# Low parts of four weight chunks: adding DMA transfers onto ScalarE's negative high parts instead of VectorE's subtraction

## The chip, the cores and the metric

The kernel runs on one core of a Trainium2 chip. The metric is the device time of one execution in microseconds (us), given as the median of several runs. TensorE (PE) multiplies matrices; VectorE (DVE), ScalarE (ACT) and GpSimd (POOL) do elementwise work; SyncE (SP) issues transfers. Each of these has an instruction queue of its own that runs in order and waits on semaphores. Transfers issued by SP, ACT or POOL are carried out by 16 DMA engines.

## The reference

A decoder trunk of two layers on 256 tokens with width 1024, in float32:

```
for layer in (0, 1):
    h = h + 0.5 * swiglu(rms_norm(h), ffn1)     # 1024 -> 2816 -> 1024
    h = h + mixer[layer](rms_norm(h))
    h = h + 0.5 * swiglu(rms_norm(h), ffn2)
out = rms_norm(h) * final_norm
swiglu(x) = (silu(x @ w_gate) * (x @ w_up)) @ w_down
```

The first layer's mixer joins a dilated window attention and a spatial gating. The second layer's is an attention with 16 heads of 64; with 256 tokens and blocks of 256 it is plain causal attention. Its output is projected by `c_w_out` (1024 x 1024), and the last FFN (`ffn2` of layer 1) follows.

## The kernel before

**Arithmetic.** A float32 value `x` is used as a high part `hi`, which is `x` rounded to the matmul format float32r, and a low part `lo = x - hi`. Each product is three matmuls (`mm3`, L283 to L285): high by high, and two of high by low. TensorE does little else than these, 7617 matmuls.

**Weights.** All weight matrices are cut into 165 chunks of up to 128 x 2048 float32 (1024 KB). `Stream` carries each through three steps: `load_one` (L146) has SP load it into one of three `raw` tiles; `split_parts` makes `whi` (ScalarE, a copy that rounds, L188) and `wlo` (VectorE, `raw - whi`, L189), in two halves of 1024 columns for an ordinary chunk; then TensorE uses both. `whi` and `wlo` have four buffers each (`SPL`). A `raw` tile is free for the next load when the last instruction that reads it is done.

**Order.** The program is written in the order in which TensorE wants its work, and a scheduler orders the instructions of each engine by that order and by its own estimate of when they are ready. Where a split shouldn't come before something else on its engine, the code says so: `hold` stops splitting, `release(tc, behind, one)` lets one chunk or all go, with an edge that puts its instructions behind the given ones on the same engine, and `split_first` starts a chunk with its first half alone.

**The second mixer's end.** In `c_mixer` a table of slots puts scores, turned probabilities and weighted sums between the projection's matmuls. The scores are masked and reduced on VectorE (L788, L803), exponentiated on ScalarE (L806), scaled by VectorE (L813), turned by TensorE (L822), split into `pth` (ScalarE) and `ptl` (VectorE, L288), and multiplied with the values; `mixh` and `mixl` (L836, L838) are the result's two parts. `project` multiplies them with four chunks of `c_w_out`: two that hold two row blocks over all columns, then two that hold the last four row blocks over one half of the columns. The splits of the latter two, and of the next FFN's first gate and up chunk, are placed by

```
slots.at((23,), lambda _: st.release(tc, [*weighted(4), *put_ks[7]], True))
slots.at((25,), lambda _: st.release(tc, weighted(5), True))
slots.at((27,), lambda _: st.split_first(tc, turn(15)))
slots.at((29,), lambda _: st.release(tc, weighted(7)))
```

After the projection `Next.pair` adds each pair of column blocks to the residual (L329), and makes the next FFN's input `xTh` (ScalarE, L319) and `xTl` (VectorE, L322). The FFN's first chunk is used in the order `TURNS`: row blocks 0 to 3, then 4 and 5, then 6 and 7; the second in plain order. ScalarE also issues a load of the final norm's gains (`fg`, L539) at the FFN's start, and POOL has the power of the root (L291) some time later.

Of the kernel before, what the change touches and what calls it, by code (L numbers as in the profile page):

```python
# [10 lines left out]
F32 = mybir.dt.float32  # L11
F32R = mybir.dt.float32r
AF = mybir.ActivationFunctionType
ALU = mybir.AluOpType
# [22 lines left out]
LINE, SHIFT = 64, 16  # L37
EDGE, GAP = 56, 240

RESET, RESHIFT = 3, 52  # L40
DOWN = ((0, 8), (8, 8), (16, 6))
MIX1, MIX2 = (4, 5, 6, 7, 0, 1, 2, 3), (0, 1, 2, 3, 4, 5, 6, 7)


def weight_chunks():

    chunks = []

    def add(m, r, n, c0, c1, shift=0, cuts=(), reset=0):
        chunks.append((m[:-1], m[-1], r, n, c0, c1, shift, cuts, reset))  # L50

    def cols(m, c0, w, cuts=(), reset=0):
        n = CH // w
        for k in range(0, KD, n):
            add(m, k * 128, n, c0, c0 + w, SHIFT if w == 256 else 0, cuts, reset)

    def ffn(name, layer, last=False, again=(2, 3)):
        first = len(chunks)
        for c in range(0, FF, 256):
            if len(chunks) == 0:  # L60
                for k in (0, 4):
                    add((f"{name}_w_gate", f"{name}_w_up", layer), k * 128, 4, c, c + 256, SHIFT,
                        (1, 2, 3) if k else (0.5, 1, 2, 3))
                continue
            for m in ("gate", "up"):
                n = len(chunks)
                cuts = (6,) if first == 0 and n in again else ()
                cols((f"{name}_w_{m}", layer), c, 256, cuts, RESET if n - first in again else 0)
        wd = (f"{name}_w_down", layer)
        if last:  # L70
            for k in range(0, FT, 2):
                add(wd, k * 128, 2, 0, D)
            return
        for c in range(0, D, 256):
            for k, n in DOWN:
                add(wd, k * 128, n, c, c + 256, SHIFT)

    def mix(m, order):
        for k in order[:4:2]:
            add(m, k * 128, 2, 0, D, SHIFT)  # L80
        for c in (0, 512):
            add(m, order[4] * 128, 4, c, c + 512, SHIFT)

    ffn("ffn1", 0, again=(2,))
    wab = ("ab_w_in", 0)
    cols(wab, 0, 256)
    cols(wab, 512, 256, reset=RESET)
    cols(wab, 1024, 512)
    cols(wab, 2048, 512)
    for c, n in ((1536, RESET), (1792, 0), (256, RESET), (768, RESET)):  # L90
        cols(wab, c, 256, reset=n)
    mix(("ab_w_out", 0), MIX1)
    ffn("ffn2", 0, again=(2,))
    ffn("ffn1", 1, again=())
    wc = ("c_w_in", 0)
    for c in range(4):
        cols(wc, c * 256, 256, reset=RESET if c % 2 else 0)
        cols(wc, 1024 + c * 256, 256, reset=0 if c else RESET)
        if c % 2 == 0:
            cols(wc, 2048 + c * 256, 512)  # L100
    mix(("c_w_out", 0), MIX2)
    ffn("ffn2", 1, True, again=(2,))
    return chunks


def loads_of(j):

    return 4 if j < 2 else 2 if j < 4 else 1
# [12 lines left out]
class Stream:  # L121
# [7 lines left out]
        self.held = False  # L129
        self.begun = None  # L130

    def add(self, nk, w, shift, cuts, reset):

        cuts = (*(cuts or (() if reset else (nk / 2,))), nk)
        self.specs.append((nk, w, loads_of(len(self.specs)), shift, cuts, reset))

    def load_one(self, between=lambda i: None):
        j = self.loaded
# [24 lines left out]
    def split_parts(self):  # L163
        j = self.split
        nc = self.nc
        nk, w, _, shift, cuts, reset = self.specs[j]
        raw = self.raws.pop(j)
        his, los = (p.tile([128, CH + LINE], F32R, name=m) for p, m in ((self.hi_pool, "whi"), (self.lo_pool, "wlo")))

        h = w // 2  # L170
        far = nk * w - reset * h + RESHIFT // LINE * LINE + RESHIFT

        def at(k):
            return int(k * w) - reset * h + shift

        def part(t, k):
            if k >= reset:
                return t[:, at(k) : at(k) + w]
            return Halves(*(t[:, a : a + h] for a in (far + k * h, shift + k * h)))

        self.parts[j] = tuple([part(t, k) for k in range(nk)] for t in (his, los))

        def split(a, r):
            n = r.free_size()
            hi, lo = his[:, a : a + n], los[:, a : a + n]
            if len(r.shape) == 3:
                hi, lo = (t.rearrange("p (k c) -> p k c", k=reset) for t in (hi, lo))
            nc.scalar.activation(hi, r, AF.Copy)  # L188
            nc.vector.tensor_sub(lo, r, hi.bitcast(F32))  # L189

        if reset:
            r = raw[:, : reset * w].rearrange("p (k c) -> p k c", k=reset)
            split(far, r[:, :, :h])
            split(shift, r[:, :, h:])
        k0 = reset
        for k1 in cuts:
            split(at(k0), raw[:, int(k0 * w) : int(k1 * w)])
            k0 = k1
            yield
        self.split += 1  # L200
# [40 lines left out]
def trunk(ctx: ExitStack, tc: tile.TileContext, a, out):  # L241
# [15 lines left out]
    for ms, _, _, n, c0, c1, *how in weight_chunks():  # L257
        st.add(n, len(ms) * (c1 - c0), *how)
# [798 lines left out]
def _layout(a):  # L1057

    def tiles(m):
        return m.reshape(-1, 128, m.shape[-1]).transpose(1, 0, 2)  # L1060

    chunks = weight_chunks()
    weights = np.zeros((len(chunks), 128 * CH), np.float32)
    for j, (ms, layer, r, n, c0, c1, *_) in enumerate(chunks):
        w = np.concatenate([a[m][layer, r : r + n * 128, c0:c1] for m in ms], axis=1)
        if j >= len(chunks) - FT // 2:
            w = w[:, ROWS]
        w = tiles(w).reshape(128, loads_of(j), -1).transpose(1, 0, 2)
        weights[j, : w.size] = w.ravel()
    norms = np.stack([a[n] for n in ("ffn1_norm", "mix_norm", "ffn2_norm")]).reshape(-1, 128)  # L1070
    x = np.zeros((KD // 2, 128, XW), np.float32)
    for i, to in enumerate(x):
        to[:, 16:] = tiles(a["x"][0].T)[:, 2 * i : 2 * i + 2].reshape(128, -1)
        to[:, :2] = norms[2 * i : 2 * i + 2].T
    pieces = x[0][:, :XFIRST], x[0][:, XFIRST:], x[1:]
    return {
        "x": np.concatenate([v.ravel() for v in pieces]),
        "norms": norms.T[:, KD:],
        "weights": weights,
        "spatial": a["ab_w_spatial"][0].transpose(2, 0, 1),  # L1080
        "ab_v_norm": a["ab_v_norm"],
        "ab_b_spatial": a["ab_b_spatial"],
        "final_norm": a["final_norm"][ROWS],
        "consts": _constants(),
    }
# [19 lines left out]
```

## Time and profile before

| | |
|---|---|
| median of 3 runs | 933.38 us (933.0 to 934.26) |
| the profiled execution | 933.77 us, of it the span of the profile 932.1 us |
| granted TensorE clock | 1.00 |
| busy: PE, DVE, ACT, POOL | 923.5, 631.2, 504.6, 76.4 us |
| DMA | 176.99 MB, 190 GB/s over the span |

A row of a timeline gives the start and the duration in us, the engine, the source line, the operation, what is written from what, how often, and in square brackets the engine's idle time before it with the instruction that ended it. A row of the waits gives who waited for whom, the sum in us, the number of times, and the longest. A row of the groups gives busy time and mean duration in ns, then the idle time before. The chain that ended last gives shares of the span.

### The profile page before, as it was taken

To read this page: it belongs to the slowest core of one execution; us is meant where nothing else is said; L and a number is where in the kernel's file an instruction comes from. 1 tells how busy PE (TensorE), PEld (TensorE's weight loads), DVE (VectorE), ACT (ScalarE), POOL (GpSimd) and SP (SyncE) were. 2 spreads that over 40 slices of the span, in tenths; PEclk is the share of its full clock that TensorE was granted. 3 is DMA by queue.
4 is the path that set the end of the run, shared out by engine and by line. 5 is a ranking of instruction groups with operands and counts; after the bars stand their busy time and mean duration, and the time that the engine had idled before them with its cause. 6 is when DMAs were issued, how large, how long until landed. Compare 5 with 4: busy or idle time off the path is not lost.

```text
span 932.1 us, 18056 instructions
## 1 busy us (share of the span) xinstructions
PE 923.5 (99%) x7617; PEld 903.1 (97%) x7617; DVE 631.2 (68%) x927; ACT 504.6 (54%) x778; POOL 76.4 (8%) x113
## 2 busy tenths in 40 slices
PE   9999999999999999999999999999999999999997
PEld 9999999999999999999999999999999999999886
DVE  7975656677888766565776655576788897656543
ACT  7754445478667554444464444456776666445431
POOL 0000000043300000000000000002664000000000
PEclk9999999999999999999999999999999999999999
DMA  9665554564246555545556554556432468555521
GB/s 328 262 226 186 190 191 165 220 224 181 92 181 226 206 202 181 196 171 203 200 195 212 182 190 179 192 193 210 171 143 91 158 236 294 195 191 208 190 91 46
DMA packets 28737, 176.99 MB, mean 190 GB/s; under 512 B 3312, under 2 KB 4976, under 8 KB 9584
## 3 DMA queue, kind: packets, MB, share of 16 engines
q1 hardware_dynamic: 27216, 173.51, 52.1%
q10 hardware_dynamic: 1440, 2.32, 0.7%
q8 instruction: 60, 0.98, 0.4%
q14 instruction: 21, 0.17, 0.0%
HBM read 173.72 MB, written 2.10 MB: 189 GB/s over the span
## 4 chain that ended last, share of the span: by engine, by line
PE 96%; DVE 2%; issue 1%; ACT 1%; DMA 0%; POOLq 0%; POOL 0%; ACTq 0%; DVEq 0%
PE bank L283 29%; PE bank L284 29%; PE bank L285 29%; PE bank L631 2%; PE bank L634 2%; PE bank L630 2%; PE bank L822 1%; PE bank L508 0%; PE bank L509 0%; PE bank L511 0%; DMA x<-in_x 0%; DVE xTl L322 0%; ACT pr L806 0%; DVE x L329 0%; DVE wlo L189 0%
## 5 line engine op out<-in xcount | busy, mean ns | idle before, releaser
L188 ACT ACTIVATE whi<-raw 128x1024 fp32r<-128x1024 f32 (+5 forms) x346 | 329.9, 999 | 336.1 <-issue 275.1
L189 DVE TENSOR_TENSOR wlo<-raw,whi 128x1024 fp32r<-128x1024 f32 (+5 forms) x346 | 389.5, 1159 | 112.7 <-ACT whi L188 111.8
L283 PE MATMUL bank<-xTh,whi 128*128 128x256 f32 x1600 | 442.9, 277 | 0.0
L284 PE MATMUL bank<-xTl,whi 128*128 128x256 f32 x1600 | 442.1, 276 | 0.1
L285 PE MATMUL bank<-xTh,wlo 128*128 128x256 f32 x1600 | 441.9, 276 | 0.0
L284 PEld LDWEIGHTS bank<-xTl,whi 128*128 128x128 f32 x1600 | 300.3, 188 | 0.3 <-DVE xTl L322 0.3
L283 PEld LDWEIGHTS bank<-xTh,whi 128*128 128x128 f32 x1600 | 300.4, 188 | 0.0
L285 PEld LDWEIGHTS bank<-xTh,wlo 128*128 128x128 f32 x1600 | 300.4, 188 | 0.0
L283 PE MATMUL bank<-hTh,whi 128*128 128x256 f32 x528 | 145.7, 276 | 0.0
L284 PE MATMUL bank<-hTl,whi 128*128 128x256 f32 x528 | 145.7, 276 | 0.0
L285 PE MATMUL bank<-hTh,wlo 128*128 128x256 f32 x528 | 145.7, 276 | 0.0
L284 PEld LDWEIGHTS bank<-hTl,whi 128*128 128x128 f32 x528 | 99.1, 188 | 0.0
L283 PEld LDWEIGHTS bank<-hTh,whi 128*128 128x128 f32 x528 | 99.1, 188 | 0.0
L285 PEld LDWEIGHTS bank<-hTh,wlo 128*128 128x128 f32 x528 | 99.1, 188 | 0.0
L570 DVE TENSOR_TENSOR hm<-gs,bank 128x512 f32<-128x512 f32 x44 | 30.1, 687 | 73.2 <-PE bank L285 71.1
L567 DVE TENSOR_TENSOR gs<-bank,row 128x512 f32<-128x512 f32 x44 | 30.3, 690 | 44.9 <-PE bank L285 44.7
L717 POOL MEMSET k<- 64x256 f32 x12 | 3.2, 306 | 566.2 <-ACT whi L188 379.6
L283 PE MATMUL bank<-mixh,whi 128*128 128x256 f32 x128 | 35.7, 279 | 0.0
L285 PE MATMUL bank<-mixh,wlo 128*128 128x256 f32 x128 | 35.4, 276 | 0.0
L284 PE MATMUL bank<-mixl,whi 128*128 128x256 f32 x128 | 35.4, 276 | 0.0
L813 POOL TENSOR_SCALAR pr<-pr,rl 128x128 f32<-128x128 f32 (+1 forms) x36 | 32.0, 900 | 30.1 <-DVE rl L809 22.9
L806 ACT ACTIVATE pr<-pr,nm 128x128 f32<-128x128 f32 (+1 forms) x48 | 21.3, 445 | 19.4 <-DVE nm L803 19.3
(172 smaller groups left out, 916.4 us busy)
## 6 DMA issues: line engine op xcount, KB each, us to landing
raw<-in_weights SPq DMA_DIRECT2D x149, 1024.0 KB, 4.9
raw<-in_weights SPq DMA_DIRECT2D x12, 768.0 KB, 4.4
raw<-in_weights SPq DMA_DIRECT2D x8, 256.0 KB, 5.0
raw<-in_weights SPq DMA_DIRECT2D x4, 512.0 KB, 6.5
away<-xn SPq DMA_DIRECT2D x2, 512.0 KB, 7.7
xr<-away SPq DMA_DIRECT2D x8, 128.0 KB, 5.8
x<-in_x SPq DMA_DIRECT2D x3, 264.0 KB, 4.8
fg<-in_final_norm ACTq DMA_DIRECT2D x1, 512.0 KB, 4.5
```

What stands on the lines that cost most here:

```text
L188: nc.scalar.activation(hi, r, AF.Copy)
L189: nc.vector.tensor_sub(lo, r, hi.bitcast(F32))
L283: nc.tensor.matmul(p, sh, mh, start=start, stop=False)
L284: nc.tensor.matmul(p, sh, ml, start=False, stop=False)
L285: nc.tensor.matmul(p, sl, mh, start=False, stop=stop)
L567: nc.vector.tensor_mul(g, both(pg), twice(norm["row"]))
L570: nc.vector.tensor_mul(hm, g, both(pu))
L630: nc.tensor.matmul(banks[t, h], sh, w[0][kw][:, cs], start=k == 0, stop=False)
L631: nc.tensor.matmul(banks[t, h], sh, w[1][kw][:, cs], start=False, stop=False)
L634: nc.tensor.matmul(banks[t, h], sl, w[0][kw][:, cs], start=False, stop=k == FT - 1)
L806: power = nc.scalar.activation(pr[:, cs], pr[:, cs], AF.Exp, bias=nm[:, b : b + 1], scale=-1.0, accum_out=l[:, b : b + 1])
L813: share = engine.tensor_scalar(pr[:, cs], pr[:, cs], rl[:, b : b + 1], None, op0=ALU.mult)
```

## The change

Four chunks get a mark `summed`: the last two of `c_w_out` and the first gate and the first up chunk of the last FFN. For each half of a marked chunk, ScalarE writes the negative high part into the low part's tile (a copy with scale -1, rounded as `whi` is), and POOL issues a transfer that adds the float32 weights from DRAM to it. VectorE's subtraction is left out. The high part and everything after it stay as they were; the other 161 chunks too.

```diff
-    def mix(m, order):
+    def mix(m, order, summed=False):
         for k in order[:4:2]:
             add(m, k * 128, 2, 0, D, SHIFT)
         for c in (0, 512):
-            add(m, order[4] * 128, 4, c, c + 512, SHIFT)
+            add(m, order[4] * 128, 4, c, c + 512, SHIFT, summed=summed)
...
-    mix(("c_w_out", 0), MIX2)
-    ffn("ffn2", 1, True, again=(2,))
+    mix(("c_w_out", 0), MIX2, True)
+    ffn("ffn2", 1, True, again=(2,), summed=(0, 1))
...
             nc.scalar.activation(hi, r, AF.Copy)
-            nc.vector.tensor_sub(lo, r, hi.bitcast(F32))
+            if summed:
+                nc.scalar.activation(lo, r, AF.Copy, scale=-1.0)
+                src = self.weights[j, : 128 * nk * w].rearrange("(p c) -> p c", p=128)
+                c0 = a - shift
+                nc.gpsimd.dma_start(lo, src[:, c0 : c0 + n], accum_op=ALU.add)
+            else:
+                nc.vector.tensor_sub(lo, r, hi.bitcast(F32))
```

The rest of the diff hands `summed` from `ffn`, `cols` and `add` of `weight_chunks` to `split_parts`.

More of the change, by code (lines that the diff above doesn't have):

```diff
@@ L47, in weight_chunks, with add, cols, ffn @@
     chunks = []
-    def add(m, r, n, c0, c1, shift=0, cuts=(), reset=0):
-        chunks.append((m[:-1], m[-1], r, n, c0, c1, shift, cuts, reset))
-    def cols(m, c0, w, cuts=(), reset=0):
+    def add(m, r, n, c0, c1, shift=0, cuts=(), reset=0, summed=False):
+        chunks.append((m[:-1], m[-1], r, n, c0, c1, shift, cuts, reset, summed))
+    def cols(m, c0, w, cuts=(), reset=0, summed=False):
         n = CH // w
         for k in range(0, KD, n):
-            add(m, k * 128, n, c0, c0 + w, SHIFT if w == 256 else 0, cuts, reset)
-    def ffn(name, layer, last=False, again=(2, 3)):
+            add(m, k * 128, n, c0, c0 + w, SHIFT if w == 256 else 0, cuts, reset, summed)
+    def ffn(name, layer, last=False, again=(2, 3), summed=()):
         first = len(chunks)
@@ L67, in ffn @@
                 cuts = (6,) if first == 0 and n in again else ()
-                cols((f"{name}_w_{m}", layer), c, 256, cuts, RESET if n - first in again else 0)
+                cols((f"{name}_w_{m}", layer), c, 256, cuts, RESET if n - first in again else 0, n - first in summed)
         wd = (f"{name}_w_down", layer)
@@ L130, in __init__, with add @@
         self.begun = None
-    def add(self, nk, w, shift, cuts, reset):
+    def add(self, nk, w, shift, cuts, reset, summed):
         cuts = (*(cuts or (() if reset else (nk / 2,))), nk)
-        self.specs.append((nk, w, loads_of(len(self.specs)), shift, cuts, reset))
+        self.specs.append((nk, w, loads_of(len(self.specs)), shift, cuts, reset, summed))
     def load_one(self, between=lambda i: None):
@@ L165, in split_parts @@
         nc = self.nc
-        nk, w, _, shift, cuts, reset = self.specs[j]
+        nk, w, _, shift, cuts, reset, summed = self.specs[j]
         raw = self.raws.pop(j)
```

## The prediction

> **What bounds the kernel now.** I read the page first: busy shares, then the chain that ended last.
>
> ```profile
> span 932.1 us, 18056 instructions
> ...
> PE 923.5 (99%) x7617; PEld 903.1 (97%) x7617; DVE 631.2 (68%) x927; ACT 504.6 (54%) x778; POOL 76.4 (8%) x113
> ...
> PE 96%; DVE 2%; issue 1%; ACT 1%; DMA 0%; POOLq 0%; POOL 0%; ACTq 0%; DVEq 0%
> ```
>
> TensorE is busy 923.5 of 932.1 us and makes up 96% of the chain. A faster VectorE can only give back what TensorE waits for. So the second view is the list of TensorE's waits over the whole run, and after it the TensorE timeline near the second mixer's end, where two of the four fall.
>
> ```profile
> PE bank L493 <- DVE warm L485: 1.1, 1, 1.1
> PE bank L283 <- DVE nm L803: 0.8, 1, 0.8
> PE bank L283 <- DVE ptl L288: 0.3, 1, 0.3
> PE bank L508 <- ACT whi L188: 0.2, 1, 0.2
> ```
>
> ```profile
> 723.31 0.47 PE L283 MATMUL bank<-pth,vth 128*128 128x512 f32 x1 [0.76 <-DVE nm L803]
> ...
> 733.05 0.47 PE L283 MATMUL bank<-pth,vth 128*128 128x512 f32 x1 [0.28 <-DVE ptl L288]
> ```
>
> The first and last of the four waits belong to the start of the kernel. The others, 0.76 + 0.28 = 1.04 us, stand where the change works, and this is nearly all that it can win: 0.11% of the time. The VectorE timeline there shows why they exist.
>
> ```profile
> 719.61 2.36 DVE L189 TENSOR_TENSOR wlo<-raw,whi 128x1024 fp32r<-128x1024 f32 x2 [0.23 <-ACT whi L188]
> 722.00 0.49 DVE L788 TENSOR_TENSOR added<-bank,mask 128x128 f32<-128x128 f32 x2
> ...
> 729.96 2.35 DVE L189 TENSOR_TENSOR wlo<-raw,whi 128x1024 fp32r<-128x1024 f32 x2
> 732.35 1.95 DVE L288 TENSOR_TENSOR ptl<-bank,pth 128x384 fp32r<-128x384 f32 x4
> 734.21 1.22 DVE L189 TENSOR_TENSOR wlo<-raw,whi 128x1024 fp32r<-128x1024 f32 x1
> ...
> 738.84 3.50 DVE L189 TENSOR_TENSOR wlo<-raw,whi 128x1024 fp32r<-128x1024 f32 x3 [0.23 <-ACT whi L188]
> 742.37 1.29 DVE L329 TENSOR_TENSOR x<-bank,x 128x512 f32<-128x512 f32 x2
> ...
> 745.04 0.87 DVE L322 SCALAR_TENSOR_TENSOR xTl<-x,gT,xTh 128x256 fp32r<-128x256 f32 x2
> ```
>
> Subtractions of weight chunks (L189) stand ahead of the score work at 722.00, of the turned probabilities' low parts at 732.35 and of the residual adds at 742.37. In program order these are the two halves of the third output chunk (719.61), those of the fourth (729.96), one half of the first gate chunk (734.21) and, at 738.84, its other half and both halves of the first up chunk: exactly the four chunks of the change. They make the eight instructions of this view (lines by form, 718 to 743 us):
>
> ```profile
> L189 DVE TENSOR_TENSOR wlo<-raw,whi 128x1024 fp32r<-128x1024 f32 x8 | 9.4, 1219 | 0.5 <-ACT whi L188 0.5
> ...
> L188 ACT ACTIVATE whi<-raw 128x1024 fp32r<-128x1024 f32 x8 | 8.0, 1053 | 0.0
> ```
>
> **Part 1: off VectorE.** Eight subtractions go, 9.4 us. The score work of 722.00 could start 2.36 us earlier, which covers the 0.76 us wait; the one of 732.35 loses its own 2.35 us, which covers 0.28 us, if ScalarE keeps up.
>
> **Part 2: onto ScalarE.** Eight negative copies come, each as long as the high part's copy beside it: 8.0 us in all. Its timeline shows whom they delay.
>
> ```profile
> 718.52 2.01 ACT L188 ACTIVATE whi<-raw 128x1024 fp32r<-128x1024 f32 x2
> 722.85 0.40 ACT L806 ACTIVATE pr<-pr,nm 128x128 f32<-128x128 f32 x1 [2.32 <-DVE nm L803]
> ...
> 726.01 0.40 ACT L806 ACTIVATE pr<-pr,nm 128x128 f32<-128x128 f32 x1 [1.30 <-DVE nm L803]
> ...
> 728.71 1.99 ACT L188 ACTIVATE whi<-raw 128x1024 fp32r<-128x1024 f32 x2
> 730.73 1.64 ACT L288 ACTIVATE pth<-bank 128x384 fp32r<-128x384 f32 x4
> ...
> 736.95 0.77 ACT L836 ACTIVATE mixh<-bank 64x256 fp32r<-64x256 f32 x2 [1.64 <-PE bank L285]
> 737.75 2.96 ACT L188 ACTIVATE whi<-raw 128x1024 fp32r<-128x1024 f32 x3
> 743.10 0.91 ACT L319 ACTIVATE xTh<-x,gT 128x256 fp32r<-128x256 f32 x2 [2.39 <-DVE x L329]
> ```
>
> The third chunk's two copies fit the 2.32 us idle before 722.85: 718.52 + 4.0 = 722.5, no later than now. The fourth chunk's come ahead of the four probability copies of 730.73. But the score exponentials before them, fed by VectorE earlier, start 0.35 sooner and lose the 1.30 idle ahead of 726.01: the chunk starts at 728.71 - 0.35 - 1.30 = 727.1 and the probability copies at 731.1, 0.4 later than now. VectorE, free then, follows within one instruction (1.95 / 4 = 0.49): two copies, 0.8, and one low part, near 732.4; now the second low part is there at 732.35 + 0.97 = 733.3. I take both waits as gone, 1.04 us. If the exponentials don't move up, the copies come at 732.7 and nothing is won at the second wait.
>
> The last three pieces come behind the mixer's last copies (736.95), which come with TensorE 1.0 us sooner: 735.9 + 0.8 + twice 2.96 = 742.6 (or 742.9, if only the first wait goes), where ScalarE can begin with the scaled copies of 743.10. VectorE's adds no longer hold them, ScalarE's own queue does. So this point moves by 0.2 to 0.5 us, not by 1.0. In the trace the third feature block's low part is made from 745.04 and is done at 745.48; TensorE uses it at 745.72 (with it, the first uses of the low parts in question):
>
> ```profile
> 731.47 0.28 PE L285 MATMUL bank<-mixh,wlo 128*128 128x256 f32 x1
> ...
> 738.36 0.28 PE L285 MATMUL bank<-mixh,wlo 128*128 128x256 f32 x1
> ...
> 745.72 0.28 PE L284 MATMUL bank<-xTl,whi 128*128 128x256 f32 x1
> ...
> 747.90 0.28 PE L285 MATMUL bank<-xTh,wlo 128*128 128x256 f32 x1
> ...
> 750.77 0.28 PE L285 MATMUL bank<-xTh,wlo 128*128 128x256 f32 x1
> ...
> 752.19 0.28 PE L285 MATMUL bank<-xTh,wlo 128*128 128x256 f32 x1
> ```
>
> That low part comes to about 745.0 to 745.3, so TensorE is ahead by 0.45 to 0.75 us from there: I take **0.6 us**, and nothing more from the stage's later, smaller slacks.
>
> **Part 3: eight transfers.** POOL issues them; it has nothing else to do here (0.00 busy from 719.4 until its next instruction, the 759.30 row: a wait for VectorE, not for these), so nothing is queued behind their waits on ScalarE:
>
> ```profile
> 759.30 0.78 POOL L291 TENSOR_TENSOR rstd<-ms,half_neg 128x2 f32<-128x2 f32 x1 [39.89 <-DVE ms L364]
> ```
>
> SP's loads are no longer released by the subtraction but by the second negative copy: 722.5 instead of 722.0, 731 for 732.3, 738.8 for 740.1, 742.7 for 742.4. That is no cost. What decides is when the low parts land. The last three rows of the TensorE fence are the first uses of the gate chunk's second half and of the up chunk's halves; 0.6 us earlier they are due at **747.3, 750.2 and 751.6**. Their negative copies end at about 738.8, 740.7 and 742.7. The DMA view from 739 to 750 us shows what else runs then (40 slices of 0.275 us):
>
> ```profile
> DMA  0000000924988999999498999978998954431000
> ...
> q1 hardware_dynamic: 288, 2.10, 51.3%
> q10 hardware_dynamic: 144, 0.52, 12.0%
> ...
> raw<-in_weights SPq DMA_DIRECT2D x2, 1024.0 KB, 5.5
> fg<-in_final_norm ACTq DMA_DIRECT2D x1, 512.0 KB, 4.5
> ```
>
> ```profile
> 740.10 2.60 SPq L146 DMA_DIRECT2D raw<-in_weights  x2
> ```
>
> The two loads take 51.3% of 11 us, 5.64, so 2.82 us of all 16 engines each; the 512 KB of the gains 12.0%, 1.32. The engines are full from 740.9, 0.8 after the issue of 740.10, to about 747. A plain 512 KB costs half a load, 1.41. No row has an adding transfer. Low bound 1.41 (the add is free); high bound 4.2 (three passes: source, old values, result). It is nearest to the load, in which bytes cross an engine twice (in, out); here they cross three times, so 1.5 x 1.41 = **2.1 us**.
>
> With lead 0.8 and equal turns between the queues: gate's second half and SP's first load share from 739.6; the half is done at 743.8, the load at 745.2. The up chunk's first half runs from 743.8 beside the load, then beside the second load and the gains (from 745.3): done 749.2. Its second half runs beside those two, then alone: done 752.9. About 0.5 us to landing (the gains: last busy slice near 749.2, landed 745.25 + 4.5 = 749.75): 744.3, 749.7, 753.4 against 747.3, 750.2, 751.6. Only the last is late, by 1.8 us. At 1.41 none is late; at 2.8 the up chunk's halves are late by 2.5 and 1.4; at 4.2 all three, by 2.4 + 2.9 + 2.8 = 8.1. The five earlier transfers: the third chunk's first half, negative at 720.5, is due at 731.47 - 0.76 = 730.7; the fourth's, at 729.1, at 738.36 - 1.04 = 737.3. They have 8 us and more each, beside one load at most, and cost nothing up to about 4 us a piece.
>
> **Sum.** -0.6 + 1.8 = +1.2 us on the profiled execution's 933.77 us (span 932.1), which is 0.39 above the median of 933.38: **934.6 us**. 0.2% is 1.9 us, about what a measurement here can tell from no change.
>
> One rule weighed: the trace has no adding transfer, so nothing here shows it yet. The Trainium skill, "Collectives: The Full Stack", section "The bandwidth ceiling: the fold count and why AG ≠ RS ≠ AR", says that a transfer which adds is slower not for the addition but because it reads two sources through one read ring, and gives half the rate. By that the piece would cost twice 1.41 and the sum would be the first rival's.
>
> **Rivals.**
> 1. Adding costs two full passes or more (2.8 us a piece, up to 4.2). For it: the engines are 94% full just then, and each piece must fetch weights and old values. Against it: part of the reading is from on-chip memory, and the loads might yield. Late by 3.9: -0.6 + 3.9 = +3.3, 936.7 us; at 4.2, +7.5, 940.9.
> 2. The transfers' start is slow (descriptors made by POOL in software, which no row shows) or a piece takes 6 us and more, so the earlier chunks are late too. At 10 us each, the eight would end near 720.6 + 80 = 801, 49 us too late. Decided from about 4 us a piece. 942 us and more.
> 3. Faster: the transfers land in time, both waits go, and the matmul spacing recovers. Between 750.77 and 752.19 TensorE starts 12 matmuls in 1.42 us, 0.118 each; between 745.72 and 747.90 19 in 2.18, 0.115. If the later adds no longer disturb it, some 60 matmuls win 0.2 us. Against it: ScalarE's queue holds the first feature blocks. -1.04 - 0.2 = 932.1 us. More than 1.9 us would need a gain that I find no row for.
> 4. Nothing happens: ScalarE's extra 8 us put the waits back where VectorE's were, and the transfers land: 933.4 us.
>
> Rival 1 is the one on the other side of my forecast: it is decided by one number, the engine time of a piece, and turns into "slower" at about 2.35 us (by the same turns as above: late by 2.5).
>
> **Chances.** Forecast (a piece of up to 2.3 us; 932.5 to 935.2) 0.40; rival 1, 0.34; rival 2, 0.11; rival 3, 0.10; rival 4, 0.05. Faster by over 0.2%: half of rival 3, 0.05. Within: forecast, rival 4 and the rest of rival 3, 0.50. Slower: rivals 1 and 2, 0.45. The range 932.0 to 939.5 leaves out a part of rival 3, rival 2 and rival 1's end near 4.2.
>
> **What would show it.** The two waits at 723 and 733 gone; whi and negative copies alternating on ScalarE, in this order, until about 742.7; SP's first load near 738.8. Eight POOL issues; their queue's share per piece gives the 2.1. A TensorE wait in the second chunk of the last FFN (750 to 756), its releaser a DMA, of 1.8 us. It would be wrong if the order on ScalarE is another (negative copies put behind the scaled copies would move the landings by 2 us and more), if SP's loads give way, or if a piece costs nearer to a plain copy or to three.

## Result: 943.1 us, slower by 1.0%

| | median, us | runs | against before |
|---|---|---|---|
| before | 933.44 (933.0 to 934.26) | 4 | |
| after | 943.1 (942.14 to 943.87) | 4 | 1.0102 (95%: 1.0084 to 1.0119) |

The forecast was 934.6 us with a range of 932.0 to 939.5; the time lies 3.6 us above its upper end. The profiled execution after took 943.87 us with a span of 942.1 us: 10.0 us more than the span before.

**Profile after.** TensorE's waits over the whole run:

```profile
PE bank L291 <- DMA wlo<-in_weights: 5.3, 4, 3.1
PE bank L289 <- DVE ptl L294: 1.8, 1, 1.8
PE bank L499 <- DVE warm L491: 1.1, 1, 1.1
PE bank L514 <- ACT whi L188: 0.4, 1, 0.4
```

(The changed kernel's lines are six higher: matmuls L289 to L291, `ptl` L294; the negative copy is L190, the transfer L193.) The wait for `nm` is gone. The one for `ptl` grew from 0.3 to 1.8 us. A new one has come, for the transfers, four times. Its four rows in TensorE's timeline, with a few more, show that the engine also ran slower behind two of the waits:

```profile
733.79 0.47 PE L289 MATMUL bank<-pth,vth 128*128 128x512 f32 x1 [1.81 <-DVE ptl L294]
...
735.78 0.41 PE L289 MATMUL bank<-mixh,whi 128*128 128x256 f32 x1
735.99 0.41 PE L290 MATMUL bank<-mixl,whi 128*128 128x256 f32 x1
...
743.34 0.38 PE L291 MATMUL bank<-mixh,wlo 128*128 128x256 f32 x1 [1.15 <-DMA wlo<-in_weights]
...
752.69 0.38 PE L291 MATMUL bank<-xTh,wlo 128*128 128x256 f32 x1 [0.61 <-DMA wlo<-in_weights]
...
758.80 0.54 PE L291 MATMUL bank<-xTh,wlo 128*128 128x256 f32 x1 [3.12 <-DMA wlo<-in_weights]
759.14 0.42 PE L289 MATMUL bank<-xTh,whi 128*128 128x256 f32 x1
...
762.12 0.46 PE L291 MATMUL bank<-xTh,wlo 128*128 128x256 f32 x1 [0.42 <-DMA wlo<-in_weights]
```

After the waits of 1.81 and 3.12 us the matmuls start 0.21 us apart and last 0.41 for some 3 us, where they otherwise start 0.113 apart and last 0.28. The table by stretches (length, then PE, PEld, DVE, ACT, POOL busy, then granted clock, DMA share and GB/s) gives the same as a clock:

```profile
735.00:740.00 5.00, 5.00 (x30) 4.82 (x29) 0.88 (x3) 2.41 (x6) 0.85 (x1) 0.66 1.04 288
...
745.00:750.00 5.00, 5.00 (x45) 5.00 (x44) 4.42 (x9) 4.52 (x10) 0.99 (x2) 1.00 0.99 260
```

At 0.66 TensorE is "busy" for all 5 us and yet does 30 matmuls; from 745 to 750, at 1.00, it does 45. A busy share alone would hide this loss.

**Where the 10.0 us lie.** I paired every matmul of after with the same one of before and followed how far it is shifted. By place: -0.9 at 723 (the wait that went), +1.46 at 733, +1.45 behind it at half rate, +1.4 at the first use of the fourth chunk's second half (743.34), +0.86, +3.24 and +0.9 at the gate chunk's second half and the up chunk's halves (752.69, 758.80, 762.12), +1.1 at half rate between the last two, and the rest, about +0.5, in small steps, 0.2 of it ahead of 715. From 763 to the end nothing changes any more. In groups: late transfers 6.4, half rate 2.6, the work before the transfers +0.6.

**Why the transfers are late.** The DMA view from 720 to 766 us, in which the work of all eight lies:

```profile
DMA  0059999999797999999999899999999999999999
...
q0 software_dynamic: 1152, 4.19, 51.3%
q1 hardware_dynamic: 957, 7.06, 40.3%
...
raw<-in_weights SPq DMA_DIRECT2D x7, 1024.0 KB, 8.8
wlo<-in_weights POOLq DMA_DIRECT2D x8, 512.0 KB, 10.2
```

The POOL queue's 4.19 MB took 51.3% of 46 us: 23.6 us for eight pieces, 2.95 us each on average. SP's 7.06 MB, 1.7 times as many bytes, took 40.3%. From 725 us on the engines are nearly full: their share is 0.89 to 1.07 in every stretch of 5 us up to 765. The queues don't take equal turns: between 732.9 and 736.3 us the trace shows packets of POOL's queue alone (97.3% of the engines), the first half of the fourth chunk, although SP issued a load at 732.56. This load landed 9.5 us after its issue, where 4.9 is the median of such loads in the kernel before. That one piece took about 4 us of the engines. The issues on POOL:

```profile
730.94 0.86 POOL L193 DMA_DIRECT2D wlo<-in_weights  x1 [7.21 <-ACT wlo L190]
732.83 0.86 POOL L193 DMA_DIRECT2D wlo<-in_weights  x1 [1.04 <-ACT wlo L190]
...
742.38 0.86 POOL L193 DMA_DIRECT2D wlo<-in_weights  x1 [5.14 <-ACT wlo L190]
744.26 0.86 POOL L193 DMA_DIRECT2D wlo<-in_weights  x1 [1.03 <-ACT wlo L190]
746.16 0.86 POOL L193 DMA_DIRECT2D wlo<-in_weights  x1 [1.04 <-ACT wlo L190]
```

and, in the view of the transfer's line, the time from issue to landing:

```profile
DMA to landing us min/median/max: 5.9/10.2/15.9
```

POOL comes 0.3 us after the copy and is at it for 0.86 us; where no earlier piece is in the way, the first packets follow about 2 us after the copy's end. Then the pieces issued at 742.38, 744.26 and 746.16, 1.9 us apart at 2.95 us each and with loads beside them, fall further behind one after another: they landed 10.3, 14.5 and 15.9 us after their issue.

**Why the wait on `ptl` grew.** ScalarE's timeline, then VectorE's:

```profile
725.94 0.40 ACT L812 ACTIVATE pr<-pr,nm 128x128 f32<-128x128 f32 x1 [1.63 <-DVE nm L809]
...
732.56 1.64 ACT L294 ACTIVATE pth<-bank 128x384 fp32r<-128x384 f32 x4
```

```profile
723.53 0.17 DVE L815 RECIPROCAL rl<-l 128x2 f32<-128x2 f32 x1 [2.15 <-ACT pr L812]
723.73 0.55 DVE L819 TENSOR_SCALAR pr<-pr,rl 128x128 f32<-128x128 f32 x2
...
725.07 0.48 DVE L794 TENSOR_TENSOR added<-bank,mask 128x128 f32<-128x128 f32 x2
...
733.08 1.95 DVE L294 TENSOR_TENSOR ptl<-bank,pth 128x384 fp32r<-128x384 f32 x4 [3.33 <-ACT pth L294]
```

VectorE is early, but its order is fixed: the next scores (725.07), whose matmuls start by 722.48, stand behind the scaling of the last ones, which waits 2.15 us for ScalarE's exponentials, and these had first to let the third chunk's negative copies by. They start at 722.45 in place of 722.85. Of these 0.4 us only 0.07 arrive at the next exponentials (725.94 in place of 726.01), because VectorE now does both of the next masked adds ahead of the reduction that feeds them, where before one filled a gap behind a reciprocal and the other came behind the reduction. The fourth chunk's two negative copies then put the probability copies to 732.56 in place of 730.73.

### The profile page after: what moved, and what is told of

Read it like the earlier page. It is cut to its first block, busy times and chain, and to the rows that moved or that the text cites. A ratio compares the mean times of both kernels' runs of the same rounds, so it can differ in the third digit from the quotient of the medians.

```text
span 942.1 us, 18072 instructions
## 1 busy us (share of the span) xinstructions
PE 927.2 (98%) x7617; PEld 905.8 (96%) x7617; DVE 622.0 (66%) x919; ACT 511.5 (54%) x786; POOL 83.6 (9%) x121
## 3 DMA queue, kind: packets, MB, share of 16 engines
q0 software_dynamic: 1152, 4.19, 2.5%
## 4 chain that ended last, share of the span: by engine, by line
PE 92%; ACT 2%; DMA 2%; DVE 1%; issue 1%; SPq 0%; POOLq 0%; POOL 0%; ACTq 0%; DVEq 0%
PE bank L291 28%; PE bank L289 28%; PE bank L290 28%; PE bank L636 2%; PE bank L640 2%; PE bank L637 2%; DMA wlo<-in_weights 2%; ACT whi L188 1%; ACT wlo L190 1%; PE bank L828 1%; DMA raw<-in_weights 1%; ACT pr L812 0%; DVE xTl L328 0%; PE bank L514 0%; PE bank L515 0%
## 5 line engine op out<-in xcount | busy, mean ns | idle before, releaser
L195 DVE TENSOR_TENSOR wlo<-raw,whi 128x1024 fp32r<-128x1024 f32 (+5 forms) x338 | 380.0, 1158 | 112.3 <-ACT whi L188 111.5
L291 PE MATMUL bank<-xTh,wlo 128*128 128x256 f32 x1600 | 442.9, 277 | 4.2 <-DMA wlo<-in_weights 4.2
L289 PE MATMUL bank<-xTh,whi 128*128 128x256 f32 x1600 | 443.5, 277 | 0.0
L291 PEld LDWEIGHTS bank<-xTh,wlo 128*128 128x128 f32 x1600 | 300.9, 188 | 4.8 <-DMA wlo<-in_weights 4.8
L289 PEld LDWEIGHTS bank<-xTh,whi 128*128 128x128 f32 x1600 | 301.0, 188 | 0.0
L289 PE MATMUL bank<-hTh,whi 128*128 128x256 f32 x528 | 145.7, 276 | 0.0
L291 PE MATMUL bank<-hTh,wlo 128*128 128x256 f32 x528 | 145.7, 276 | 0.0
L291 PEld LDWEIGHTS bank<-hTh,wlo 128*128 128x128 f32 x528 | 99.1, 188 | 0.0
L289 PEld LDWEIGHTS bank<-hTh,whi 128*128 128x128 f32 x528 | 99.1, 188 | 0.0
L291 PE MATMUL bank<-mixh,wlo 128*128 128x256 f32 x128 | 36.1, 282 | 1.2 <-DMA wlo<-in_weights 1.2
L289 PE MATMUL bank<-mixh,whi 128*128 128x256 f32 x128 | 36.4, 284 | 0.0
L637 PE MATMUL bank<-wlo,hTh 128*128 128x512 f32 x80 | 31.1, 389 | 0.0
```

What stands on the lines that cost most here:

```text
L289: nc.tensor.matmul(p, sh, mh, start=start, stop=False)
L291: nc.tensor.matmul(p, sl, mh, start=False, stop=stop)
L637: nc.tensor.matmul(banks[t, h], sh, w[1][kw][:, cs], start=False, stop=False)
```

## Experiments

Eleven kernels. Medians stand beside those of before, taken on the same chip at the same time; edits are against the changed kernel, and a kernel whose edit drops the negative copies has them dropped for all marked chunks. Experiments 1, 2, 3, 7 and 8 leave some low parts incomplete; they are for timing alone.

**1. No transfers.** The three lines of the transfer are taken out.

```diff
             nc.scalar.activation(lo, r, AF.Copy, scale=-1.0)
-            src = self.weights[j, : 128 * nk * w].rearrange("(p c) -> p c", p=128)
-            c0 = a - shift
-            nc.gpsimd.dma_start(lo, src[:, c0 : c0 + n], accum_op=ALU.add)
```

> The changed kernel without its eight adding transfers; the negative copies on ScalarE stay, so the low parts of the four chunks are left as negative high parts and their weights are wrong. Theory A (three separate costs: ScalarE's copies ahead of the probability copies, the transfers' engine time, and TensorE at half rate after a long wait): the 0.76 us wait at 723 is gone, the wait at 733 grows to 1.8 us as in the changed kernel, and half rate follows it for some 3 us (+1.5), nothing else: 933.4 - 0.9 + 1.5 + 1.5 = 935.5 us. Theory B (ScalarE's extra work is what costs, the transfers only look late because they start late): most of the 9.7 us stays, 940 us or more. Theory C (the half rate comes from the busy DMA engines, not from the wait): the wait at 733 stays, but matmuls after it are 0.114 us apart: 934.0 us.

934.77 us against 933.88, ratio 1.0013 (1.0004 to 1.0022). Of the 9.7 us, the transfers make 8.8; ScalarE's part is left:

```profile
PE bank L286 <- DVE ptl L291: 1.8, 1, 1.8
```

The profile shows that wait without half rate behind it; two of the ten runs, with a granted clock of 0.997 rather than 0.999, took 1.4 and 2.2 us more than the median. The expected 935.5 us counted on half rate in every run, and it came in few.

**2. Plain transfers.** Same issues, order and bytes, without the adding.

```diff
-            nc.gpsimd.dma_start(lo, src[:, c0 : c0 + n], accum_op=ALU.add)
+            nc.gpsimd.dma_start(lo, src[:, c0 : c0 + n])
```

> The changed kernel with plain transfers in place of the adding ones: same bytes from DRAM, same queue, same waits, but the weights replace the negative copies, so the low parts are wrong. Theory A: a piece takes 1.4 to 1.6 us of the engines instead of 2.9, and lands before its use; only the wait at 733 and the half rate after it are left: 935.5 to 936.5 us, as without transfers. Rival D (what is late is the start, by POOL's issue and the software queue, not the engine time): the waits at the last FFN's second chunk keep most of their 5 us: 940 us or more.

935.93 us against 933.88, ratio 1.0022 (1.0013 to 1.0031). The same DMA view, 720 to 766 us, and the waits:

```profile
q0 software_dynamic: 1152, 4.19, 28.5%
...
wlo<-in_weights POOLq DMA_DIRECT2D x8, 512.0 KB, 6.3
```

```profile
PE bank L291 <- DMA wlo<-in_weights: 0.3, 1, 0.3
```

28.5% of 46 us is 13.1, 1.64 us a piece. The wait for `ptl` is 1.8 us as before, and TensorE waits for the transfers 0.3 us. POOL's issues are shorter here, 0.53 us in place of 0.86; experiment 3 has them at 0.86 again.

**3. Half the bytes, with adding.**

```diff
-            nc.gpsimd.dma_start(lo, src[:, c0 : c0 + n], accum_op=ALU.add)
+            nc.gpsimd.dma_start(lo[:, : n // 2], src[:, c0 : c0 + n // 2], accum_op=ALU.add)
```

> As the changed kernel, with the same eight adding transfers issued at the same points, but each brings only the first half of its piece's columns (256 KB in place of 512 KB; the other half of each low part stays the negative high part, so low parts aren't the reference's). Theory A (a piece is late because it holds the engines for 2.93 us and shares them with the loads): at half the bytes a piece costs about 1.5 us of the engines, as the plain transfers did, so it lands 4 to 9 us after its issue, TensorE waits for low parts of the last FFN for at most 1 us in all, and the time is 935 to 937 us. Rival (an adding transfer has a long way of its own, whatever its size: it reads the old values back first, or waits behind other traffic by its count of packets): landings stay at 10 to 16 us after the issue for the last pieces and the time stays at 940 to 943 us.

937.25 us against 933.8, ratio 1.0037 (1.0026 to 1.0048), the profiled run 935.36. The same DMA view:

```profile
q0 software_dynamic: 1152, 2.10, 28.3%
...
wlo<-in_weights POOLq DMA_DIRECT2D x8, 256.0 KB, 7.4
```

Half the bytes with adding cost as much as all of them without, 1.63 us a piece, and land after 4.1 to 9.4 us. TensorE waits 0.4 us for them in the profiled run. POOL's issues and the slow start are those of the changed kernel, so neither is the cost by itself, and an adding transfer has no long way of its own: it is late by the engines' time that it takes. The median lies just above the expected 937; the runs spread over 3.2 us, and what the longer ones lose more has no profile.

**4 and 5. Only the output projection's chunks; only the FFN's.**

```diff
-    ffn("ffn2", 1, True, again=(2,), summed=(0, 1))
+    ffn("ffn2", 1, True, again=(2,))
```

> Only the two chunks of c_w_out by adding transfers. Theory A: -0.9 (first wait) + 1.5 (wait at 733) + 1.5 (half rate) + 0.5 to 1.4 (fourth chunk's second half, which competes with one load and one piece fewer) = +2.5 to +3.5: 936 to 937 us. Theory B: about half of the 9.7 us, as half of the copies: 938 us.

```diff
-    mix(("c_w_out", 0), MIX2, True)
+    mix(("c_w_out", 0), MIX2)
```

> Only the first gate and up chunk of the last FFN by adding transfers. Theory A: the waits at 723 and 733 are back as in the kernel before, and the gate chunk's second half and the up chunk's halves are late by 5 to 6 us in all, with half rate after the longest (+1.2): 939.5 to 941 us. Theory B: about half of the 9.7 us: 938 us.

936.75 us, ratio 1.0038 (1.0023 to 1.0053), and 941.59 us, ratio 1.0078 (1.0062 to 1.0095), both against 933.88. The losses, 2.9 and 7.7, add up to 10.6 where both together lose 9.7. The second is a little more than the expected 941. Its four pieces alone make TensorE wait 5.0 us, where the same pieces make 4.2 of the 5.3 in the changed kernel, so the pieces of the other two chunks aren't what delays them:

```profile
PE bank L291 <- DMA wlo<-in_weights: 5.0, 3, 3.1
...
PE bank L289 <- DVE nm L809: 0.7, 1, 0.7
```

**6. Only the third chunk.** As 4, and the mark for the third chunk alone.

```diff
-            add(m, order[4] * 128, 4, c, c + 512, SHIFT, summed=summed)
+            add(m, order[4] * 128, 4, c, c + 512, SHIFT, summed=summed and c == 0)
```

> Only the third chunk of c_w_out by adding transfers (its pieces were in time in the changed kernel). Theory A: the wait at 723 goes (-0.9), but the later scores' exponentials stay at 726, so the fourth chunk's split and the probabilities' low parts stay at 732.3 and TensorE waits there for what it won: -0.2 to -0.4, 933.3 to 933.7 us. Theory of the prediction (the exponentials move up with VectorE): -0.9 to -1.0, 932.7 us.

933.36 us against 933.74, ratio 0.9996 (0.9987 to 1.0004). The wait at 723 is gone, but the one at 733 grows from 0.3 to 0.9 us:

```profile
PE bank L289 <- DVE ptl L294: 0.9, 1, 0.9
```

TensorE comes there 1.0 us earlier, but the probabilities' low parts are begun only 0.3 us earlier (732.03 in place of 732.35), so two thirds of the gain go back at the next wait.

**7. A longer wait, no transfers.** As 1, with the fourth chunk's negative copies made twice.

```diff
-            nc.scalar.activation(lo, r, AF.Copy, scale=-1.0)
+            for _ in range(2 if j == 131 else 1):
+                nc.scalar.activation(lo, r, AF.Copy, scale=-1.0)
```

> As x1 (no transfers; low parts of the four chunks left as negative high parts), with the fourth chunk's negative copies made twice: the wait at 733 grows from 1.8 to some 3.7 us. Theory A (half rate follows a long enough wait, with a chance that grows with its length): 934.8 + 1.9 for the wait + 1.5 or more for half rate in all runs: 938 to 939 us, clock 0.997 or less in each. Theory C (half rate needs busy DMA engines): 936.7 us, clock 0.999.

937.57 us against 933.74, ratio 1.0045 (1.0031 to 1.0059), granted clock 0.996 or 0.997 in all four runs. TensorE's timeline:

```profile
735.46 0.79 PE L287 MATMUL bank<-pth,vth 128*128 128x512 f32 x1 [3.35 <-ACT pth L292]
736.05 0.41 PE L287 MATMUL bank<-mixh,whi 128*128 128x256 f32 x1
736.26 0.41 PE L288 MATMUL bank<-mixl,whi 128*128 128x256 f32 x1
...
738.61 0.31 PE L289 MATMUL bank<-mixh,wlo 128*128 128x256 f32 x1
738.76 0.28 PE L287 MATMUL bank<-mixh,whi 128*128 128x256 f32 x1
738.88 0.28 PE L288 MATMUL bank<-mixl,whi 128*128 128x256 f32 x1
```

Half rate comes without a transfer: it follows the wait, and ends some 3.1 us after it. The time is a little below the expected 938.

**8. A shorter wait, no transfers.** As 1, but the fourth chunk's second low part is made by GpSimd.

```diff
-            nc.scalar.activation(lo, r, AF.Copy, scale=-1.0)
+            if j == 131 and a > shift:
+                nc.gpsimd.tensor_sub(lo, r, hi.bitcast(F32))
+            else:
+                nc.scalar.activation(lo, r, AF.Copy, scale=-1.0)
```

> As the kernel with the negative copies and no transfers (low parts of the four chunks aren't the reference's), but the second half of the output projection's fourth chunk has its low part made by a subtraction on GpSimd, so ScalarE has one copy (1.0 us) less ahead of the turned probabilities' copies. These come near 731.6 and TensorE's wait there falls from 1.8 to about 0.8 us or less. Theory A (TensorE runs at half rate for about 3 us after a wait there if the wait is long enough; 1.8 us does it in some runs, 3.4 us in all): here in none, clock 0.999 in all runs, 933.3 to 933.9 us. Rival (half rate comes by itself in some runs, whatever the wait): again about one run in five at clock 0.997, some 1.5 us longer, with a median of 934.3 or more.

933.68 us against 933.76, ratio 0.9998 (0.9989 to 1.0007), clock 0.998 to 1.0 in all ten runs, the wait 0.9 us:

```profile
PE bank L289 <- DVE ptl L294: 0.9, 1, 0.9
```

With 1, 2, 3, 4 and 7 this is a ladder of the wait and the clock: 0.9 us, 0.997 or less in 0 of 10 runs; 1.8 us, in 2 of 10, 4 of 10, 1 of 8 and 4 of 4 (all but the first with transfers); 3.35 us, in 4 of 4. The wait is that of the profiled run.

**What decides at 1.8 us.** The traces record when the granted clock changes. In the changed kernel this is at 734.99, 738.40, 758.88 and 762.29 us: half rate comes in stretches of 3.41 us, and the two begin seven times 3.41 apart. In every profiled run the changes lie on such a grid of windows, counted from the change to full clock in its first 7 us, and the grid lies elsewhere in each run. These are the windows around the wait of 1.81 us in the changed kernel, in experiment 1 and in experiment 3 (columns as in the table by stretches):

```profile
731.58:734.99 3.41, 1.60 (x10) 1.13 (x9) 1.91 (x4) 3.39 (x7) 1.07 (x2) 1.00 0.82 89
734.99:738.40 3.41, 3.41 (x17) 3.31 (x16) 0.89 (x3) 1.71 (x4) 0.85 (x1) 0.50 1.03 280
```

```profile
729.04:732.46 3.42, 2.85 (x26) 2.65 (x24) 0.61 (x2) 3.41 (x4) 0.00 (x0) 1.00 0.00 0
732.46:735.87 3.41, 2.17 (x14) 1.89 (x15) 1.95 (x4) 3.40 (x7) 0.00 (x0) 1.00 0.67 226
735.87:739.28 3.41, 3.41 (x28) 3.21 (x27) 1.67 (x4) 2.35 (x6) 0.00 (x0) 1.00 0.22 87
```

```profile
729.68:733.10 3.42, 1.95 (x18) 1.75 (x16) 0.37 (x1) 3.40 (x6) 1.48 (x2) 1.00 0.30 46
733.10:736.51 3.41, 3.07 (x20) 2.76 (x21) 1.69 (x5) 3.26 (x6) 0.72 (x2) 1.00 1.03 265
736.51:739.92 3.41, 3.41 (x28) 3.24 (x28) 1.58 (x4) 2.53 (x4) 0.37 (x1) 1.00 1.02 229
```

In the changed kernel the whole wait falls into one window, which leaves TensorE idle for 1.81 of 3.41 us, and the next window is at 0.50. In experiments 1 and 3 a border cuts the same wait, into 0.57 and 1.24 and into 1.47 and 0.34, and no window is slowed. The other profiled runs agree: windows at full clock with 1.81 idle (experiment 4), 2.39 (experiment 5), 3.12 (the changed kernel) and 3.15 (experiment 7) are followed by half rate, and windows with 1.15 or less aren't. So between 1.47 and 1.81 us of idle time in one window are needed, and for a wait of 1.8 us the place of the grid decides. From half rate the way back may need more: in experiment 5 a slowed window with 1.38 idle was followed by a second one. Busy DMA engines are neither needed (share 0.00 in experiment 7's idle window) nor enough (1.03 and 1.02 above, at full clock). The runs without a profile have only their mean clock, so their place on the grid isn't known.

**9. GpSimd subtracts, all four chunks.** No copies, no transfers.

```diff
-                nc.scalar.activation(lo, r, AF.Copy, scale=-1.0)
-                ...
-                nc.gpsimd.dma_start(lo, src[:, c0 : c0 + n], accum_op=ALU.add)
+                nc.gpsimd.tensor_sub(lo, r, hi.bitcast(F32))
```

> The four chunks' low parts by POOL's subtraction: no negative copies, no transfers, ScalarE as in the kernel before. Theory A (what was wrong with the change is ScalarE's copies and the transfers, not the move off VectorE): both waits at 723 and 733 go, low parts are in time at some 3 us a piece: -1.0 to -1.8, 931.7 to 932.6 us. Rival E: VectorE and POOL slow each other, and nothing is won: 933.5 to 934.5 us.

934.71 us against 933.74, ratio 1.0012 (1.0003 to 1.0021), more than either expectation. Both waits go (TensorE is 1.3 us ahead near 745), then it loses 2.2 us up to 752, of it 1.3 in waits for `xTl`. VectorE's timeline, then POOL's:

```profile
741.00 4.12 DVE L325 SCALAR_TENSOR_TENSOR xTl<-x,gT,xTh 128x256 fp32r<-128x256 f32 x2
```

```profile
737.54 7.29 POOL L190 TENSOR_TENSOR wlo<-raw,whi 128x1024 fp32r<-128x1024 f32 x3 [0.87 <-ACT whi L188]
```

Two operations that take 0.87 us in the kernel before take 4.12 beside GpSimd's subtraction. Looked at singly, the first ends 0.28 us after GpSimd's second piece (742.59 against 742.31), the second 0.29 after its third (745.12 against 744.83). Two scalings of probabilities at 721.38 take 2.92 in place of 0.55 in the same way. Operations that read a matmul bank are not held: the `ptl` at 730.99 take 1.95 us as ever.

**10. GpSimd subtracts, the projection's two chunks.** As 9, with the edit of 4.

> POOL's subtraction for the two chunks of c_w_out alone. Theory A: both waits go, the later splits on VectorE stay: -0.8 to -1.3, 932.3 to 932.8 us. Rival E: 933.5 to 934.5 us.

933.41 us against 933.74, ratio 0.9996 (0.9988 to 1.0005). Again a VectorE operation with both inputs in tiles, none in a matmul bank, is caught beside GpSimd, 2.33 us for 1.22. The `mixl` behind it comes late, TensorE waits 0.6 us for it, and most of the gain is gone, against the 932.3 to 932.8 that was expected:

```profile
733.65 2.33 DVE L192 TENSOR_TENSOR wlo<-raw,whi 128x1024 fp32r<-128x1024 f32 x1
```

**11. GpSimd subtracts five pieces**: the projection's two chunks and the gate chunk's first half; VectorE the other three. As 9, with one more line changed:

```diff
-            if summed:
+            if summed and not (j == 133 or j == 132 and a > shift):
```

> Low parts of the output projection's third and fourth chunk and of the first half of the first gate chunk by subtractions on GpSimd (2.4 us each, no negative copies, no transfers), the other three of the eight pieces on VectorE as in the kernel before. Theory A (GpSimd's subtractions win both waits and do harm only where VectorE has an operation on two on-chip operands at the same time; in the run with all eight this was near 741, in the run with four near 733.6): both places are cleared, so both waits go and nothing comes back: 1.0 to 1.3 us less than before, 932.4 to 932.8 us. Rival (GpSimd's third stretch, now to about 737, delays the mixed output's low parts of 734 to 737 on VectorE or the gate chunk's own first half): one of them is over a microsecond late and the gain is gone, 933.3 to 934.7 us.

932.71 us against 933.76, ratio 0.9989 (0.998 to 0.9998). Both waits are gone from the list and nothing takes their place; of the four rows of before one is left:

```profile
PE bank L496 <- DVE warm L488: 1.1, 1, 1.1
```

It wins the 1.0 us that the prediction had found to be won, without the transfers.

## Why the prediction was wrong

**What bounds the kernel: right.** At most 1.04 us was to be won, and experiment 11 won 1.05.

**Part 1, VectorE: half right.** The wait at 723 went. The one at 733 did not, and not by VectorE's fault.

**Part 2, ScalarE: wrong.** The step that failed is "the exponentials before them, fed by VectorE earlier, start 0.35 sooner and lose the 1.30 idle". The first exponentials did start 0.40 sooner, but those ahead of the fourth chunk started at 725.94, 0.07 sooner, and their idle time was 1.63. I had followed VectorE's instruction to ScalarE, but not what stands ahead of it in VectorE's order: a scaling that itself waits for ScalarE. The text named the other case (copies at 732.7; they came at 732.56) but priced it as "nothing is won at the second wait"; it costs 1.5 us more wait. The prediction's own steps gave that: copies at 732.7 put the low part at 734.0, 0.7 us later than before, and TensorE comes 0.76 earlier. Experiment 6 shows the smaller form of it, experiment 1 the whole. So "-0.6" from this part was +0.6, before any half rate.

**Part 3, the size of a piece: mis-sized.** I took 2.1 us of the engines, by counting how often bytes cross; it measured 2.95. The weighed rule had it: the Trainium skill, "Collectives: The Full Stack", section "The bandwidth ceiling: the fold count and why AG ≠ RS ≠ AR", gives the adding step of a collective half the rate of a copy; taken over to a single transfer, this makes a piece twice 1.41, 2.82 us. This trace agrees within 5% on the average of eight pieces, and experiment 3 shows the factor of two (half the bytes with adding, 1.63 us; all without, 1.64). That was rival 1, which I held for less likely by the row of the plain load alone.

**Part 3, the lead: mis-sized, and cheap by itself.** 0.8 us from release to first packets, taken from SP's loads; POOL's took about 2. Experiment 3 has the same issues and, with pieces of 1.63 us, a wait of 0.4 us. What the lead adds to pieces of 2.95 us no run separates.

**Part 3, "they have 8 us and more each ... and cost nothing up to about 4 us a piece": wrong.** The fourth chunk's second half, its copy done at 732.54, landed at 743.30 and cost 1.4 us at 2.95 a piece, although TensorE came for it only 9.7 us after the copy. I had priced the first halves alone: the second stood behind its own chunk's first half, whose packets went until about 737, then ran beside SP's load, and its copy came later than forecast.

**The waits in the last FFN: in the right place, of the wrong size.** Forecast 1.8 us, for the up chunk's second half alone; measured 5.0 over three pieces, by the shifts above. Experiment 5 has 5.0 too, with copies 0.8 to 0.9 us later than forecast. Rival 1 at 2.8 us a piece gave 3.9 by the same turns, so most of the error is the price of a piece. The turns were not equal, as the load of 732.56 shows; that 3.9 came near has some luck in it.

**What had no term: half rate.** 2.6 us. Experiments 7 and 8 and the windows behind them show that it comes with TensorE's wait and not with the DMA. The Trainium skill, "TensorE: Matmul & The Clock Gate", section "Part 1: The HAM clock gate (the "warmup" mystery)", tells of a gate that halves the clock after an idle window of about 3.4 us, with windows that run freely. The half rate and the free windows, 3.41 us long, are as it says; the idle time that is enough isn't: here a window with 1.81 us idle did it, and one with 1.47 did not. That is why, in the profiled runs, a wait of 1.8 us slows some and not others.

Put together, rival 1's 936.7 had the mechanism and missed the rest: 1.2 us from the score work, 1.4 from the fourth chunk, 1.1 in the FFN and 2.6 at half rate make 6.3 of the 6.7 that the span lost beyond its +3.3.

## What to carry to other kernels

Before moving work from a busy engine to the DMA engines, price the transfer in engine time and not in bytes: one that adds cost 1.8 times a plain one by the same queue here, and where the engines are full the pieces pile up. To see whether an instruction moves up, follow what stands ahead of it on each engine's queue until you come back to your own engine; slack that runs in a circle isn't slack. And a wait of TensorE of two or three microseconds can have a second price, 3.4 us at half rate, some 1.5 us lost, so its cost can be nearly twice what the list of waits says.

## What the hardware showed that I had not expected

- An adding transfer of 512 KB took 2.95 us of the 16 engines on average, a plain one by the same queue 1.64.
- Half rate for one window of 3.41 us (matmuls 0.21 us apart rather than 0.113) behind a window in which TensorE was idle for 1.81 us or more. With 1.47 us idle it did not come.
- A VectorE operation whose inputs are all in tiles, none in a matmul bank, was held until GpSimd's subtraction beside it ended: 4.12 us for 0.87, 2.92 for 0.55, 2.33 for 1.22. The profile books the blocked time as busy time of VectorE, so it looks like a slow operation and not like a wait.
